# First loads of a two-layer decoder trunk issued at once; the squares of its first norm put behind the casts

## The chip, the cores and the metric

The kernel runs on one core of a Trainium2 chip. Its time is device time in microseconds (us) of one whole execution; lower is better. Three executions of the kernel before took 1265.56 us (median), 1262.03 us and 1266.27 us. A fourth, recorded by the hardware profiler, took 1263.57 us; from its first to its last recorded instruction, which is called the span, 1261.8 us pass.

## The reference, cut to what matters

The input x has 512 tokens of 1024 float32 values. Two layers work on it, each of them a token mixer with a residual and a squared-ReLU MLP (hidden size 4096) with a residual, and each of these starts with an RMSNorm:

```
def rmsnorm(x, g):
    y = x * rsqrt(mean(x * x, axis=-1) + EPS) * g
for layer in range(2):
    hn = rmsnorm(h, norm_mix[layer])
    h = h + mixer(hn, w_in[layer], ...)        # layer 0: even_mixer, layer 1: odd_mixer
    h = h + square(relu(rmsnorm(h, norm_mlp[layer]) @ w1)) @ w2
return rmsnorm(h, norm_final)
```

The change touches the very first rmsnorm and the first products of the even mixer: q, k and v of four heads of differential attention and eight heads of forgetting attention, all out of one projection `hn @ w_in`, with a rotary turn of q and k of the first group. The rest (attention, gates, output projections, the top-k attention of layer 1, the MLPs) is not changed.

## The kernel before

**Layout.** Everything is held transposed: 1024 features are 8 blocks of 128 partitions, each with 512 tokens (256 KB). A product in float32 is made of three TensorE passes over numbers that are split in two (a high part that the engine takes as it is, and the rest as a low part): high times high, high times low, low times high (L325, L326, L327). One output block of 128 columns is 8 such triples over the feature blocks, 24 matmuls of 128x128 by 128x512, into one bank of PSUM called `pg`; three such banks exist (`B_PG`).

**Weights.** All weights lie in one packed array in the order in which they are used. `stage` (L250) writes the plan. `emit_split` (L257; its load is L264) takes the next entry of the plan: at the first column block of an entry it loads the raw weights on SyncE's queue into one of two `raw` buffers (512 KB for an entry of 128 columns), then ScalarE makes the high part (L160, a cast) and VectorE the low part (L161, a subtraction) into one of three `whl` buffers. `wnext` calls it one block ahead of use.

**The first norm.** `first_norm` (L225 on) loads the blocks of x (tiles `hx`), splits the first weights in two halves, and calls `norm`. For each feature block j, `norm` makes the high part of x times the norm's gain on ScalarE (L202) and the low part on VectorE (L203), lets the first product go on by a step (`step`), and then squares an earlier block on ScalarE (L209, L212) and adds the square up on VectorE (L213). The factor of rmsnorm itself is not needed for the product: it is multiplied in later. From the sum of squares, eight small matmuls (L166), VectorE (L169), GpSimd's power (L171) and VectorE (L218, L176) make a diagonal matrix, two matmuls (L189, L190) spread it over the partitions, ScalarE copies it to `r_b` (L220), and VectorE multiplies the rotary tables `csr` by it (L223). Only then can the first product's bank `pg` be read out (L360, L361) and be used for the fourth output block.

**Before the first norm** TensorE runs `WARM` matmuls on a tile of ones (L130) whose result nothing reads.

**Order.** The program is written in the order above, but a planner of the framework fixes the order of each engine's instructions at build time: by its own costs it walks through time, and of the instructions whose inputs it takes to be ready on an engine, it puts the one that the program names first. The engines then run that fixed order, each one strictly in line. DMA issues of a queue stand in the same line as the engine's own work: the queue of ScalarE carries x blocks of odd number, `cols` and `ident`; that of SyncE the even ones, the weights and `csr`. The framework has a small number of completion counters for these DMAs, so that a late issue first waits until an earlier DMA has landed.

Of the kernel before, what the change touches and what calls it, by code (L numbers as in the profile page):

```python
# [13 lines left out]
AF = mybir.ActivationFunctionType  # L14
# [7 lines left out]
KB = D // P  # L22
# [27 lines left out]
V_FIRST = 2  # L50
DVE_ODD = 6
DVE_EVEN = 6
WARM = 8
PAD = 320
SHUF = list(range(8, 16)) + list(range(0, 8)) + list(range(16, 32))
OFF = [P * t * (t + 1) // 2 for t in range(NT + 1)]
# [22 lines left out]
def trunk(ctx, tc, packs, b_forget, lambda_q1, lambda_k1, lambda_q2, lambda_k2, rope, eye, xT, vecs, wpk, out):  # L79
    nc = tc.nc  # L80
# [7 lines left out]
    def blk(tag, bufs, shape=(P, S), dt=F32, pool=None):  # L88
        tile_n[0] += 1
        return (pool or big).tile(list(shape), dt, name=f"{tag}_{tile_n[0]}", tag=tag, bufs=bufs)  # L90
# [9 lines left out]
    scr = lambda: blk("scr", 5)  # L100
# [5 lines left out]
    h = [lpool.tile([P, S], F32, name=f"hx{j}") for j in range(KB)]  # L106

    def load_x(j, q=None):
        (q or nc.sync).dma_start(h[j], xT[j * P:(j + 1) * P])
# [18 lines left out]
    busy = pO()  # L128
    for i in range(WARM):
        nc.tensor.matmul(busy, onesf[:, :P], onesf, start=True, stop=True)  # L130
    nhalf = const.tile([P, NT], F32, name="nhalf")
    nc.gpsimd.memset(nhalf, -0.5)
    csr = const.tile([P, 2, S], F32, name="csr")
# [25 lines left out]
    def split(dst_hi, dst_lo, src, eng=None):  # L159
        nc.scalar.copy(dst_hi, src)  # L160
        (eng or nc.vector).tensor_sub(dst_lo, src, dst_hi.bitcast(F32))  # L161

    def rsqrt_cols(sq, inv_n, ts=range(NT)):
        p = pT()
        for t in ts:
            nc.tensor.matmul(p[:, t:t + 1], sq[:, t * P:(t + 1) * P], ones1, start=True, stop=True)  # L166
        c = slice(ts[0], ts[-1] + 1)
        v = small(4)
        nc.vector.tensor_scalar(v[:, c], p[:, c], inv_n, EPS, op0=OP.mult, op1=OP.add)  # L169
        r = small(4)  # L170
        nc.gpsimd.tensor_tensor(r[:, c], v[:, c], nhalf[:, c], op=OP.pow)  # L171
        return r
# [19 lines left out]

    rtm = const.tile([P, NT], F32, name="rtm")

    def norm(gcol, rope_tab, step=None, lag=0):
        gh = []
        acc = scr()
        for j in range(KB):
            hi = blk("gh", 16, dt=F32R)
            lo = blk("gh", 16, dt=F32R)  # L200
            g = cols[:, gcol + j:gcol + j + 1]
            nc.scalar.activation(hi, h[j], AF.Copy, scale=g)  # L202
            nc.vector.scalar_tensor_tensor(lo, h[j], g, hi.bitcast(F32), op0=OP.mult, op1=OP.subtract)  # L203
            gh.append((hi, lo))
            if step:
                step(gh)
            for i in range(max(j - lag, 0) if j >= lag else KB, j - lag + 1 if j < KB - 1 else KB):
                if i == 0:
                    nc.scalar.activation(acc, h[i], AF.Square)  # L209
                else:  # L210
                    sq = scr()
                    nc.scalar.activation(sq, h[i], AF.Square)  # L212
                    nc.vector.tensor_add(acc, acc, sq)  # L213
        r_tables(rsqrt_cols(acc, 1.0 / D), rope_tab)
        return gh

    def r_tables(r, rope_tab):
        nc.vector.tensor_copy(rtm, r)  # L218
        p = bcast_cols(r)
        nc.scalar.copy(r_b, p)  # L220
        if rope_tab:
            for i in range(2):
                nc.vector.tensor_mul(csr[:, i], csr[:, i], r_b)  # L223

    def first_norm(w, c0):  # L225

        load_x(1, nc.scalar)
        emit_split(2)
        for j in range(2, KB):
            load_x(j, nc.scalar if j % 2 else nc.sync)  # L230
        nc.sync.dma_start(csr, rope.rearrange("a p s -> p a s"))
        nc.scalar.dma_start(ident, eye)
        pout = pg()
        wt = ready.pop(0)[0]
        gen = []

        def step(gh):
            if not gen:
                gen.append(gemm_steps(pout, wt, gh))
                return  # L240
            next(gen[0])

        gh = norm(0, True, step, 2)
        for _ in gen[0]:
            pass
        return gh, pout

    plan, ready = [], []
# [5 lines left out]

    raws = {}

    def emit_split(parts=1):  # L257
        w, r0, c0, c, n, wd, lo, at = plan.pop(0)
        ks = [slice(i * KB // parts, (i + 1) * KB // parts) for i in range(parts)]
        if c == 0:  # L260
            raw = blk("raw", RAW_BUFS, (P, KB * WC), F32, wts)[:, :KB * wd]
            src = wpk[at:at + D * wd].rearrange("(p f) -> p f", p=P)
            for k in ks:
                nc.sync.dma_start(raw[:, k.start * wd:k.stop * wd], src[:, k.start * wd:k.stop * wd])  # L264
            raws[0] = raw.rearrange("p (k c) -> p k c", c=wd)
        t = blk("whl", WHL_BUFS, (P, 2, KB, P), F32R, wts)
        for k in ks:
            split(t[:, 0, k, :n], t[:, 0, k, n:2 * n] if n == 8 else t[:, 1, k, :n], raws[0][:, k, c:c + n], lo)
        ready.append((t, w, r0, c0 + c))

    def wnext(w, r0, c):
        while plan and len(ready) <= AHEAD:
            emit_split()
        t, w_, r_, c_ = ready.pop(0)
        assert (w_, r_, c_) == (w, r0, c)
        return t
# [44 lines left out]
    def gemm_steps(pout, wt, rhs, n=P, start=True, stop=True, ks=range(KB)):  # L321
        for k, (a, b) in enumerate(rhs):
            if k not in ks:
                continue
            nc.tensor.matmul(pout, wt[:, 0, k, :n], a, start=start and k == 0, stop=False)  # L325
            nc.tensor.matmul(pout, wt[:, 0, k, :n], b, start=False, stop=False)  # L326
            last_mm[0] = nc.tensor.matmul(pout, wt[:, 1, k, :n], a, start=False, stop=stop and k == KB - 1)  # L327
            yield
# [306 lines left out]
    def h_reload(ap):  # L635
        r = [blk("h", KB, pool=ap) for j in range(KB)]
        for j in range(KB):
            nc.sync.dma_start(r[j], hd[j])
        return r
# [11 lines left out]
    def mlp(ap, layer, done=None):  # L651
        gh = norm(16 + KB * layer, False)
        half = 2 * D
        w1, w2 = ("w_mlp_in", layer), ("w_mlp_out", layer)
        for f0 in range(0, D_FF, half):
            acts = []
            def fin(p, put):
                t = blk("t", 3, pool=ap)
                nc.vector.scalar_tensor_tensor(t, p, 0.0, r_b, op0=OP.max, op1=OP.mult)  # L659
                hi = blk("act", 32, dt=F32R, pool=ap)  # L660
                lo = blk("act", 32, dt=F32R, pool=ap)
                nc.scalar.activation(hi, t, AF.Square)
                sq = blk("t", 3, pool=ap)
                nc.scalar.activation(sq, t, AF.Square)
                nc.vector.tensor_sub(lo, sq, hi.bitcast(F32))
                put((hi, lo))

            for s in range(half // WC):
                acts += proj(w1, gh, f0 + s * WC, fin)
            out_gemm(w2, f0, acts, done if f0 + half == D_FF else None)  # L670
# [149 lines left out]
    def odd(ap, gh):  # L820
# [119 lines left out]
        return early.finish(obs)  # L940

    gh, p0 = first_norm(("w_in_even", 0), 0)
    load.__exit__(None, None, None)
    with tc.tile_pool(name="even", bufs=1, reuse_waits="tile") as ap:
        om, pe = even(ap, gh, p0)
    with tc.tile_pool(name="mlp0", bufs=1, reuse_waits="tile") as ap:
        blk("pad", 1, (P, PAD // 4), pool=ap)
        h = [blk("h", KB, pool=ap) for j in range(KB)]
        for j in range(KB):
            load_x(j)  # L950
        out_gemm(("w_out_even", 0), 0, om, early=pe)
        mlp(ap, 0)
        nc.scalar.dma_start(csr, rope.rearrange("a p s -> p a s"))
        gh = norm(KB, True)
        h_spill()
    with tc.tile_pool(name="odd", bufs=1, reuse_waits="tile") as ap:
        om, pe = odd(ap, gh)
    with tc.tile_pool(name="mlp1", bufs=1, reuse_waits="tile") as ap:
        blk("pad", 1, (P, PAD // 4), pool=ap)
        h = h_reload(ap)  # L960
# [48 lines left out]
```

## Time and profile before

| what | us |
|---|---|
| median of three runs | 1265.56 |
| the profiled execution | 1263.57 |
| its span | 1261.8 |
| TensorE matmuls busy | 1242.1 |
| VectorE busy | 719.8 |
| ScalarE busy | 558.9 |
| GpSimd busy | 97.6 |

Busy times add up the time in which an engine has an instruction in work. They are read as shares of the span: TensorE is at 98%. What an engine other than TensorE does counts only where TensorE waits for it, so that the stretches in which TensorE stands still, or runs at its lower clock, are what there is to read.

### The profile page before, as it was taken

The numbers are of one execution on the slowest core, as the hardware profiler recorded it, in microseconds if no ns is written. First come the engines' busy times: TensorE is split into PE (matmuls) and PEld (weight loads), VectorE is DVE, ScalarE is ACT, GpSimd is POOL, SyncE is SP. The second block draws the span as 40 slices with busy tenths as digits, with TensorE's granted clock in tenths as the row PEclk, the third lists the DMA queues.
The fourth block names the chain that finished last, engine by engine and source line by source line (L and its number), as shares of the span: only waits on it lengthen the run. The fifth ranks groups of instructions, "written<-read, shape, count | busy, mean of one in ns | idle before, by whom it ended". The sixth has DMA issues, their size and how long they took to land.

```text
span 1261.8 us, 15425 instructions
## 1 busy us (share of the span) xinstructions
PE 1242.1 (98%) x5856; PEld 1026.8 (81%) x5856; DVE 719.8 (57%) x1359; ACT 558.9 (44%) x1014; POOL 97.6 (8%) x68
## 2 busy tenths in 40 slices
PE   7999999999999999999999999999999999999997
PEld 5878888888888888888788888877888888888887
DVE  6887659664432244434499987787644322444232
ACT  5456667444421134323353578885533222333231
POOL 2000000000000000000114533230000000000000
PEclk9999999999999999999999999999999999999999
DMA  6546342322222222233334344523322222222211
GB/s 184 144 120 166 96 142 73 121 100 100 101 101 89 85 94 100 101 117 110 134 100 152 96 124 118 152 79 134 100 101 90 88 92 98 100 100 100 101 67 67
DMA packets 36298, 136.82 MB, mean 108 GB/s; under 512 B 5440, under 2 KB 5568, under 8 KB 26240
## 3 DMA queue, kind: packets, MB, share of 16 engines
q1 hardware_dynamic: 34784, 133.52, 32.5%
q10 hardware_dynamic: 1136, 1.66, 0.4%
q0 software_dynamic: 304, 0.66, 0.4%
q8 instruction: 46, 0.75, 0.2%
q14 instruction: 28, 0.23, 0.1%
HBM read 111.18 MB, written 4.19 MB: 91 GB/s over the span
## 4 chain that ended last, share of the span: by engine, by line
PE 88%; DVE 5%; ACT 3%; DMA 2%; issue 1%; POOL 0%; SPq 0%; POOLq 0%; DVEq 0%; ACTq 0%
PE pg L325 26%; PE pg L326 26%; PE pg L327 26%; PE pT L484 2%; PE pS L450 1%; PE pS L451 1%; DMA raw<-in_wpk_dram 1%; PE pO L503 1%; PE pO L502 1%; DMA hx<-in_xT_dram 1%; DVE whl L161 1%; ACT P L458 1%; PE pT L166 1%; DVE P L456 1%; PE pT L419 1%
## 5 line engine op out<-in xcount | busy, mean ns | idle before, releaser
L160 ACT CAST whl<-raw 128x1024 fp32r<-128x1024 f32 (+1 forms) x199 | 206.8, 1041 | 534.4 <-PE pg L327 484.9
L325 PE MATMUL pg<-gh,whl 128*128 128x512 f32 x1064 | 421.8, 397 | 5.1 <-ACT gh L202 3.7
L326 PE MATMUL pg<-gh,whl 128*128 128x512 f32 x1064 | 416.7, 392 | 1.0 <-DVE gh L203 0.9
L327 PE MATMUL pg<-gh,whl 128*128 128x512 f32 x1064 | 416.3, 392 | 0.6 <-DVE whl L161 0.6
L161 DVE TENSOR_TENSOR whl<-raw,whl 128x1024 fp32r<-128x1024 f32 (+2 forms) x175 | 211.5, 1209 | 181.1 <-ACT whl L160 180.9
L325 PEld LDWEIGHTS pg<-gh,whl 128*128 128x128 f32 x1064 | 200.0, 188 | 44.5 <-ACT gh L202 4.9
L327 PEld LDWEIGHTS pg<-gh,whl 128*128 128x128 f32 x1064 | 199.9, 188 | 42.3 <-DVE whl L161 1.0
L326 PEld LDWEIGHTS pg<-gh,whl 128*128 128x128 f32 x1064 | 200.1, 188 | 41.9 <-DVE gh L203 3.8
L325 PE MATMUL pg<-act,whl 128*128 128x512 f32 (+1 forms) x528 | 202.1, 383 | 0.0
L327 PE MATMUL pg<-act,whl 128*128 128x512 f32 (+1 forms) x528 | 202.0, 383 | 0.0
L326 PE MATMUL pg<-act,whl 128*128 128x512 f32 (+1 forms) x528 | 202.0, 383 | 0.0
L659 DVE SCALAR_TENSOR_TENSOR t<-pg,r_b 128x512 f32<-128x512 f32 x64 | 44.3, 691 | 156.1 <-PE pg L327 153.6
L325 PEld LDWEIGHTS pg<-act,whl 128*128 128x128 f32 x528 | 99.2, 188 | 19.5
L327 PEld LDWEIGHTS pg<-act,whl 128*128 128x128 f32 x528 | 99.2, 188 | 19.3
L326 PEld LDWEIGHTS pg<-act,whl 128*128 128x128 f32 x528 | 99.2, 188 | 19.2
L458 ACT ACTIVATE P<-P,sm 128x128 f32<-128x128 f32 (+3 forms) x128 | 71.7, 561 | 48.9 <-DVE sm L456 48.5
L612 DVE TENSOR_TENSOR h<-h,pg 128x512 f32<-128x512 f32 x46 | 31.3, 686 | 106.6 <-PE pg L327 106.6
L161 POOL TENSOR_TENSOR whl<-raw,whl 128x1024 fp32r<-128x1024 f32 x24 | 57.8, 2408 | 122.2 <-ACT whl L160 100.6
L171 POOL TENSOR_TENSOR sm<-sm,nhalf 128x4 f32<-128x4 f32 (+1 forms) x10 | 12.3, 1225 | 656.8 <-DVE sm L169 656.8
L161 DVE TENSOR_TENSOR PT<-pT,PT 128x384 fp32r<-128x384 f32 (+1 forms) x84 | 49.8, 597 | 19.9 <-ACT PT L160 19.3
L160 ACT CAST PT<-pT 128x384 fp32r<-128x384 f32 (+1 forms) x84 | 42.4, 510 | 14.3 <-PE pT L484 13.8
L484 PE MATMUL pT<-ident,P 128*128 128x128 f32 x280 | 46.5, 275 | 1.8 <-ACT P L471 0.9
(198 smaller groups left out, 1163.4 us busy)
## 6 DMA issues: line engine op xcount, KB each, us to landing
raw<-in_wpk_dram SPq DMA_DIRECT2D x78, 1024.0 KB, 4.8
raw<-in_wpk_dram SPq DMA_DIRECT2D x39, 512.0 KB, 3.9
qk<-qk SPq DMA_DIRECT2D x156, 128.0 KB, 2.3
h<-in_xT_dram SPq DMA_DIRECT2D x8, 256.0 KB, 4.7
hd<-h SPq DMA_DIRECT2D x8, 256.0 KB, 2.0
h<-hd SPq DMA_DIRECT2D x8, 256.0 KB, 4.8
out_dram<-y SPq DMA_DIRECT2D x4, 512.0 KB, 3.0
hx<-in_xT_dram SPq DMA_DIRECT2D x4, 256.0 KB, 9.0
```

The costliest lines, as they stand in the source:

```text
L160: nc.scalar.copy(dst_hi, src)
L161: (eng or nc.vector).tensor_sub(dst_lo, src, dst_hi.bitcast(F32))
L166: nc.tensor.matmul(p[:, t:t + 1], sq[:, t * P:(t + 1) * P], ones1, start=True, stop=True)
L325: nc.tensor.matmul(pout, wt[:, 0, k, :n], a, start=start and k == 0, stop=False)
L326: nc.tensor.matmul(pout, wt[:, 0, k, :n], b, start=False, stop=False)
L327: last_mm[0] = nc.tensor.matmul(pout, wt[:, 1, k, :n], a, start=False, stop=stop and k == KB - 1)
L419: nc.tensor.transpose(q[:, t * P:(t + 1) * P], y[:, t * P:(t + 1) * P], ident)
L450: nc.tensor.matmul(sp[m][:, c], qb[m][:, q], kb[0][m][:, :w], start=True, stop=False)
L458: nc.scalar.activation(o, o, AF.Exp, bias=st[m][:, t:t + 1], scale=-1.0, accum_out=st[m][:, 4 + t:5 + t])
L484: nc.tensor.transpose(p[:, o - o0 + (t - kt) * P:o - o0 + (t - kt + 1) * P], pt[:, OFF[t] + kt * P:OFF[t] + (kt + 1) * P], ident)
L612: nc.vector.tensor_add(h[j], h[j], p)
L659: nc.vector.scalar_tensor_tensor(t, p, 0.0, r_b, op0=OP.max, op1=OP.mult)
```

## The change

All loads of x and the first two halves of weights are issued ahead of the first split (`fetch` is the loading part of `emit_split`, and does nothing when it has been done). The first split's casts come behind the high part of x block 0. Within `step`, the second weights are split after the last block of x, and the load of the rotary tables is issued behind that. With `lag`, all squares come in a loop of their own behind these. Two of the eight warming matmuls go.

```diff
-WARM = 8
+WARM = 6
+    def squares(acc, j):
+        if j == 0:
+            nc.scalar.activation(acc, h[j], AF.Square)
+        else:
+            sq = scr()
+            nc.scalar.activation(sq, h[j], AF.Square)
+            nc.vector.tensor_add(acc, acc, sq)
+
-    def norm(gcol, rope_tab, step=None, lag=0):
+    def norm(gcol, rope_tab, step=None, lag=False):
...
             if step:
                 step(gh)
-            for i in range(max(j - lag, 0) if j >= lag else KB, j - lag + 1 if j < KB - 1 else KB):
-                if i == 0:
-                    nc.scalar.activation(acc, h[i], AF.Square)
-                else:
-                    sq = scr()
-                    nc.scalar.activation(sq, h[i], AF.Square)
-                    nc.vector.tensor_add(acc, acc, sq)
+            if not lag:
+                squares(acc, j)
+        for j in range(KB if lag else 0):
+            squares(acc, j)
         r_tables(rsqrt_cols(acc, 1.0 / D), rope_tab)
...
     def first_norm(w, c0):
-        load_x(1, nc.scalar)
-        emit_split(2)
-        for j in range(2, KB):
+        fetch(2)
+        for j in range(1, KB):
             load_x(j, nc.scalar if j % 2 else nc.sync)
-        nc.sync.dma_start(csr, rope.rearrange("a p s -> p a s"))
         nc.scalar.dma_start(ident, eye)
         pout = pg()
-        wt = ready.pop(0)[0]
         gen = []
         def step(gh):
-            if not gen:
+            j = len(gh)
+            if j == 1:
+                emit_split(2)
+                wt = ready.pop(0)[0]
                 gen.append(gemm_steps(pout, wt, gh))
                 return
             next(gen[0])
-        gh = norm(0, True, step, 2)
-        for _ in gen[0]:
-            pass
+            if j == KB:
+                next(gen[0])
+                emit_split()
+                nc.sync.dma_start(csr, rope.rearrange("a p s -> p a s"))
+        gh = norm(0, True, step, True)
...
+    def fetch(parts=1):
+        w, r0, c0, c, n, wd, lo, at = plan[0]
+        if c == 0 and fetched[0] != at:
+            fetched[0] = at
...
     def emit_split(parts=1):
+        fetch(parts)
         w, r0, c0, c, n, wd, lo, at = plan.pop(0)
```

## Rows read from the trace of the kernel before

**Rows 1.** The page's first part: busy time of each engine, share of the span, instructions.

```profile
PE 1242.1 (98%) x5856; PEld 1026.8 (81%) x5856; DVE 719.8 (57%) x1359; ACT 558.9 (44%) x1014; POOL 97.6 (8%) x68
```

**Rows 2.** Stretches: start to end and length; busy time per engine (instructions), clock, DMA, GB/s.

```profile
9.03:19.50 10.47, 9.43 (x24) 5.60 (x25) 9.88 (x16) 10.07 (x17) 1.65 (x3) 1.00 0.71 251
19.50:24.48 4.98, 3.63 (x19) 2.50 (x17) 3.93 (x6) 0.96 (x2) 1.90 (x1) 1.00 0.25 72
```

**Rows 3.** Waits, 0 to 60 us: who waited for whom, total us, times, longest.

```profile
PE pg L325 <- ACT gh L202: 3.7, 1, 3.7
...
PE pT L189 <- ACT scr L160: 0.8, 1, 0.8
...
PE pg L327 <- DVE whl L161: 0.6, 1, 0.6
```

**Rows 4.** Timeline of ScalarE: start, duration, line, out<-in, count, [idle before <- ended by].

```profile
7.16 0.62 ACT L160 CAST whl<-raw 128x512 fp32r<-128x512 f32 x1 [1.76 <-DMA raw<-in_wpk_dram]
...
8.25 0.72 ACT L202 ACTIVATE gh<-hx,cols 128x512 fp32r<-128x512 f32 x1 [0.48 <-issue]
8.88 0.61 ACT L209 ACTIVATE scr<-hx 128x512 f32<-128x512 f32 x1
...
17.86 1.98 ACT L160 CAST whl<-raw 128x1024 fp32r<-128x1024 f32 x2
```

**Rows 5.** DMAs issued at 0.74, 1.18, 1.65, 2.12, 7.16, 10.53: us to landing last.

```profile
hx<-in_xT_dram SPq DMA_DIRECT2D x1, 256.0 KB, 2.8
raw<-in_wpk_dram SPq DMA_DIRECT2D x1, 256.0 KB, 3.6
raw<-in_wpk_dram SPq DMA_DIRECT2D x1, 256.0 KB, 5.5
hx<-in_xT_dram SPq DMA_DIRECT2D x1, 256.0 KB, 8.4
hx<-in_xT_dram ACTq DMA_DIRECT2D x1, 256.0 KB, 8.6
raw<-in_wpk_dram SPq DMA_DIRECT2D x1, 512.0 KB, 6.9
```

**Rows 6.** Timeline of VectorE, columns as in rows 4.

```profile
11.51 0.74 DVE L203 SCALAR_TENSOR_TENSOR gh<-hx,cols,gh 128x512 fp32r<-128x512 f32 x1
...
18.12 0.75 DVE L203 SCALAR_TENSOR_TENSOR gh<-hx,cols,gh 128x512 fp32r<-128x512 f32 x1
18.79 0.68 DVE L213 TENSOR_TENSOR scr<-scr,scr 128x512 f32<-128x512 f32 x1
...
20.80 1.23 DVE L161 TENSOR_TENSOR whl<-raw,whl 128x1024 fp32r<-128x1024 f32 x1
...
29.75 0.68 DVE L361 TENSOR_TENSOR scr<-pg,csr 128x512 f32<-128x512 f32 x1
```

**Rows 7.** Timeline of TensorE's matmuls, columns as in rows 4.

```profile
1.52 3.78 PE L130 MATMUL pO<-onesf 128*128 128x512 f32 x8 [1.52 <-DVE onesf L125]
...
9.03 0.79 PE L325 MATMUL pg<-gh,whl 128*128 128x512 f32 x1 [3.73 <-ACT gh L202]
...
13.39 0.63 PE L325 MATMUL pg<-gh,whl 128*128 128x512 f32 x1
13.82 0.44 PE L326 MATMUL pg<-gh,whl 128*128 128x512 f32 x1
...
19.50 0.39 PE L325 MATMUL pg<-gh,whl 128*128 128x512 f32 x1
...
24.48 0.50 PE L189 MATMUL pT<-scr,onesr 128*128 128x512 f32 x1 [0.75 <-ACT scr L160]
...
33.47 0.39 PE L327 MATMUL pg<-gh,whl 128*128 128x512 f32 x1
33.70 0.39 PE L325 MATMUL pg<-gh,whl 128*128 128x512 f32 x1
```

**Rows 8.** Waits of SyncE's queue, 0 to 60 us, columns as in rows 3.

```profile
SPq L264 <- DMA hx<-in_xT_dram: 3.4, 1, 3.4
```

More of the change, by code (lines that the diff above doesn't have):

```diff
@@ L255, in trunk, with emit_split @@
     raws = {}
[L257 to L260, printed above, removed]
+    def fetch(parts=1):
+        w, r0, c0, c, n, wd, lo, at = plan[0]
+        if c == 0 and fetched[0] != at:
+            fetched[0] = at
             raw = blk("raw", RAW_BUFS, (P, KB * WC), F32, wts)[:, :KB * wd]
             src = wpk[at:at + D * wd].rearrange("(p f) -> p f", p=P)
-            for k in ks:
-                nc.sync.dma_start(raw[:, k.start * wd:k.stop * wd], src[:, k.start * wd:k.stop * wd])
+            for k in range(parts):
+                f = slice(k * KB * wd // parts, (k + 1) * KB * wd // parts)
+                nc.sync.dma_start(raw[:, f], src[:, f])
             raws[0] = raw.rearrange("p (k c) -> p k c", c=wd)
+    fetched = [-1]
+    def emit_split(parts=1):
+        fetch(parts)
+        w, r0, c0, c, n, wd, lo, at = plan.pop(0)
         t = blk("whl", WHL_BUFS, (P, 2, KB, P), F32R, wts)
-        for k in ks:
+        for i in range(parts):
+            k = slice(i * KB // parts, (i + 1) * KB // parts)
             split(t[:, 0, k, :n], t[:, 0, k, n:2 * n] if n == 8 else t[:, 1, k, :n], raws[0][:, k, c:c + n], lo)
```

## The prediction

> **What bounds the kernel now.** The page comes first: TensorE's matmuls fill 1242.1 us, 98% of the span, so some 20 us are to be had on it, and every other engine is below 60% [rows 1]. The change touches the first 20 us and nothing behind them, so the next view is the stretches and the waits of the start. Between the first real matmul (9.03) and the end of the first product (19.50), ScalarE is busy 10.07 and VectorE 9.88 of 10.47 us: they set the pace here, not TensorE. From 19.50 to 24.48 TensorE is busy 3.63 of 4.98 us [rows 2]. Its waits name three causes: 3.7 us for the first high part of x, 0.6 us for the low part of the second weights, 0.8 us for the cast in the chain of the norm [rows 3].
>
> Why the first high part is late is seen on ScalarE: it stands at 8.25 behind the cast of the second half of the weights, which waited for its load until 7.16 [rows 4]. The load of x block 0 had landed at 0.74 + 2.8 = 3.5, the two halves of the weights at 1.18 + 3.6 = 4.8 and 1.65 + 5.5 = 7.1, x block 2 only at 2.12 + 8.4 = 10.5, x block 7 at 7.16 + 8.6 = 15.8, the second weights at 10.53 + 6.9 = 17.4 [rows 5]. VectorE then alternates a low part and an addition: six low parts start between 11.51 and 18.12, one each (18.12 - 11.51) / 5 = 1.32 us, and the sum of squares ends at 18.79 + 0.68 = 19.47 [rows 6]. The second weights' subtraction comes last, 20.80 to 22.03, and TensorE waits for it. The point by which I judge the whole start is the first matmul of the fourth output block: 33.70 [rows 7]. It needs the first bank back, which VectorE releases at 29.75 + 0.68 = 30.43 [rows 6]. So there are 33.70 - 30.43 = 3.27 us between the chain of the norm and TensorE's path: what TensorE gains up to that block is capped near 3.3 us unless the chain comes earlier too. From 33.47 to 33.70 one matmul takes 0.23 us, the pace of the rest [rows 7].
>
> **The change part by part.**
>
> *First high part in front of the casts.* ScalarE can start on x block 0 at about 3.8 (block 0 has landed, `cols` is awaited as well) in place of 8.25. The first cast can follow its load at 4.8, with 0.62 for the cast [rows 4] and about 0.7 for a subtraction of 512 columns (the addition of that size takes 0.68, [rows 6]): first matmul near 6.2, 2.8 us earlier. This is hardly worth anything by itself. TensorE does blocks 0 and 1 (six matmuls of 0.43 at the pace from 13.39 to 13.82, [rows 7]), is done near 8.8, and then waits for block 2. That load does not move: it was issued at 2.12 and is behind the same bytes. High part 0.72 [rows 4]: the low part of block 2 starts at 10.5 + 0.7 = 11.2, where it was 11.51. Gain so far 0.3 us. ScalarE's queue may put a load that waits for a counter ahead of the first high part; the last candidate frees at 7.1 (the second half's landing), and TensorE would do blocks 0 and 1 until about 10.8, still ahead of block 2's low part: 0.
>
> *x loads earlier.* The four odd blocks no longer wait behind casts. If blocks 4 to 7 (1.05 MB) move behind 10.5 at the mean 251 GB/s of this stretch [rows 2], the last lands at 14.7, between 10.5 and the old 15.8. At VectorE's pace its low part is not wanted before 11.2 + 5 x 1.32 = 17.8, or 17.6 without the small waits: 0 to 0.3 us more. I take 0.1.
>
> *Squares behind all.* The source puts them last, but the planner fills an engine when it takes the next block not to have landed. Before, a square stands right behind the first high part (8.88, [rows 4]) although the source had two more high parts ahead of it. So I expect high part and square, low part and addition to alternate again, and the first product to end near 19.1 (19.50 - 0.4).
>
> *Second weights' split ahead of the squares, their load ahead of the rotary tables.* The load was issued at 10.53 and waited 3.4 us for a counter [rows 8]; put right behind x block 6 it lands no later than 17.4, and one 512 KB load at 251 GB/s (2.1 us) earlier at best. The cast comes to ScalarE between 15.5 and 17.9, and the subtraction to VectorE right behind the last low part (18.4) or one addition later (19.1). It takes 1.23 [rows 6]: end 19.6 to 20.3 in place of 22.03, saving 1.7 to 2.4 us of TensorE's second product. That is the main term; I take 2.0.
>
> *What the norm's chain gives back.* The same subtraction now stands in front of the last additions: sum of squares at 19.47 - 0.4 + 1.15 = 20.2. The spread (L189) started at 24.48 [rows 7], 5.0 us behind the sum, and TensorE had waited for it [rows 3]; it would now start near 25.2, while TensorE comes by 2 us earlier. Its place in TensorE's line is fixed by the planner. If the planner puts enough matmuls of the second product ahead of it, this costs 0; if its place stays, the whole gain and 0.7 us are lost. The planner also sees the weights earlier, so I take the end near 0: 0.4 us.
>
> *Parts at nothing.* The rotary tables (512 KB) are issued later; they are first multiplied within the 5.95 us between 24.48 and 30.43, and landing by 17.4 + 2.1 = 19.5 leaves 5 us of cover. Without that cover each us late would be a us on the bank's release. Two warming matmuls less: eight took 3.78 us [rows 7], and TensorE stands idle behind them in any case.
>
> Sum: 0.4 + 2.0 - 0.4 - 0.4, the last for waits that the planner's new order makes further back, is 1.6 us. The profiled execution took 1263.57, so 1262.0. It lies 2.0 below the median; the four executions shown have a mean of 1264.4, and it is this that I carry the sum to: 1262.7.
>
> **The rivals.**
>
> *The planner really puts the squares behind (B).* Then a low part needs only its own 0.75. The last one ends at 16.2 (landing 14.7, high part 0.72, low part 0.75), and TensorE sets the pace: from 11.2 at 0.43 per matmul, 4.8 us long as before (9.03 to 13.82, where the pace goes up, [rows 7]), then 0.23: first product done at 17.6, second and third 48 x 0.227 = 10.9 and about 1.4 for the small ones: 29.9, a gain of 3.8. The additions end near 20.5, and 10.96 behind that (30.43 - 19.47) the bank is free: 31.5, a gain of 2.2, or more if some squares go early. I put it at 1260.5 on the same base. For it: the source's order. Against it: the square at 8.88.
>
> *Hidden anyway or taken back (C).* L189 keeps its place, or TensorE's clock rises late. The row first: eight matmuls of 0.43 from 1.52 to 5.30 did not bring the higher pace, and after 3.7 us without work TensorE began at 0.43 again, which is the level of 1.2 GHz, though the column of the clock shows 1.00 throughout [rows 2, 7]. Now it idles from about 8.8 to 11.2; if the rise comes another 4.8 us later than the 16.0 above, at 20.8, some four or five matmuls of the second product cost 0.2 us more each: 0.9 us. Then the gain is between 0 and 1.6 - 0.9 = 0.7; I take 0.5, a time of 1263.9.
>
> By the Trainium skill, "TensorE: Matmul & The Clock Gate", section "Part 1: The HAM clock gate", the half rate is what an idle engine returns to and sustained activity releases it. By that rule a start broken by a wait for block 2 keeps the lower clock longer, which is the loss of rival C; rows of before show only the unbroken start.
>
> *Slower (D): the chain of the norm becomes the path.* If ScalarE's line holds the second weights' cast (and the third's) in front of most squares, it stands for the load until 15 to 17.4, then casts 1.0, or 2.0 for two (17.86, 1.98, [rows 4]), then eight squares of 0.61 [rows 4] = 4.9: 20.9 to 24.3, and the last addition ends 0.8 later, at 21.7 to 25.1. The bank is free 10.96 later. It decides from a sum later than 33.70 - 10.96 = 22.7 on; at 25.1 the fourth block starts at 36.1, 2.4 us late. Rotated q and k, and with them the first scores, come as late. 1264.4 + 2.4 = 1266.8. For it: the order of the source; against it: squares of landed blocks fill ScalarE's line while it waits, as before.
>
> **How the numbers follow.** Forecast 0.42, B 0.26, C 0.18, D 0.14. About 0.3% (3.8 us) is what a measurement of this kernel can tell from no change. Faster by more: half or more of B, and the upper tails of the forecast, which a new order throughout the attention stage may widen: 0.30. Slower by more: most of D: 0.12. Within: 0.58. The forecast's own range is 0 to 3 us of gain, 1261.4 to 1264.4; with B, part of D and the 4.2 us by which executions of before differ, 1258.5 to 1266.5.
>
> **What would show it.** The first matmul near 6 us; a gap in TensorE before 11; high parts and squares alternating (forecast) or not (B); the subtraction of the second weights ending near 20; the fourth block starting near 32. The prediction is wrong if block 2 of x lands well before 10.5, if L189's wait grows by 2 us, or if the sum of squares ends after 22.7.

## The result, and the profile after

The changed kernel takes 1270.82 us (median of five, 1269.39 to 1270.99) against 1264.27 us of the kernel before (five, 1262.03 to 1266.27): a ratio of 1.0051, 95% interval 1.0034 to 1.0067. It is slower by 6.5 us. The forecast was 1262.7 us and the range ended at 1266.5: the time lies above both. The profiled executions, 1269.39 us and 1263.57 us, are 5.8 us apart, and so are their spans.

The page after, its first part:

```profile
span 1267.6 us, 15426 instructions
PE 1243.9 (98%) x5854; PEld 1029.2 (81%) x5854; DVE 720.1 (57%) x1359; ACT 559.2 (44%) x1014; POOL 96.3 (8%) x68
```

TensorE has nearly the same number of matmuls as in [rows 1], and its busy time grew by 1.8 us. Two stretches show where; columns as in [rows 2], the clock being the number behind the five engines. First after, then before:

```profile
34.00:43.00 9.00, 5.36 (x14) 4.20 (x14) 8.82 (x17) 2.29 (x3) 0.00 (x0) 0.65 0.49 146
...
60.00:100.00 40.00, 39.59 (x201) 31.18 (x199) 35.27 (x100) 21.56 (x49) 0.00 (x0) 1.00 0.36 101
```

```profile
34.00:43.00 9.00, 9.00 (x42) 7.44 (x41) 9.00 (x22) 2.23 (x4) 0.00 (x0) 1.00 0.66 152
...
60.00:100.00 40.00, 38.69 (x198) 30.21 (x197) 35.82 (x99) 22.53 (x51) 0.00 (x0) 1.00 0.50 134
```

From 34 to 43 us TensorE was fully busy before; now it does 14 matmuls in place of 42, stands still for 3.6 us, and its granted clock is 0.65. From 60 to 100 it gets 0.9 us back: 0.4 us of waits are left of 1.3. TensorE's timeline after shows the wait and the slow matmuls behind it (columns as in [rows 4]):

```profile
8.73 0.79 PE L341 MATMUL pg<-gh,whl 128*128 128x512 f32 x1 [4.29 <-ACT whl L160]
...
15.73 1.42 PE L341 MATMUL pg<-gh,whl 128*128 128x512 f32 x2 [2.50 <-ACT whl L160]
...
33.61 0.40 PE L343 MATMUL pg<-gh,whl 128*128 128x512 f32 x1
37.64 0.79 PE L341 MATMUL pg<-gh,whl 128*128 128x512 f32 x1 [3.64 <-DVE scr L377]
38.23 0.63 PE L342 MATMUL pg<-gh,whl 128*128 128x512 f32 x1
...
43.35 0.46 PE L342 MATMUL pg<-gh,whl 128*128 128x512 f32 x1
43.65 0.39 PE L343 MATMUL pg<-gh,whl 128*128 128x512 f32 x1
```

The last matmul of the third product starts at 33.61, only 0.14 later than in [rows 7]. Then TensorE waits 3.64 us for VectorE to read out the first bank, and the fourth block starts at 37.64 in place of 33.70: 3.94 us. Behind the wait its first 14 matmuls take 43.65 - 37.64 = 6.01 us, 0.43 each, the pace of the 1.2 GHz level; fourteen at 0.23 take 3.2. Together: 3.94 + 2.8, less the 0.9 from 60 to 100 us, and 0.2 more for waits between 43 and 60 us, is 6.0 us; the spans differ by 5.8.

Why is the bank late? VectorE after:

```profile
15.71 1.23 DVE L161 TENSOR_TENSOR whl<-raw,whl 128x1024 fp32r<-128x1024 f32 x1 [3.97 <-ACT whl L160]
16.85 0.75 DVE L211 SCALAR_TENSOR_TENSOR gh<-hx,cols,gh 128x512 fp32r<-128x512 f32 x1
...
21.91 0.75 DVE L211 SCALAR_TENSOR_TENSOR gh<-hx,cols,gh 128x512 fp32r<-128x512 f32 x1
22.57 0.68 DVE L201 TENSOR_TENSOR scr<-scr,scr 128x512 f32<-128x512 f32 x1
23.17 1.22 DVE L738 TENSOR_TENSOR pick<-ident 128x1024 fp32r<-128x1024 f32 x1
24.31 0.68 DVE L201 TENSOR_TENSOR scr<-scr,scr 128x512 f32<-128x512 f32 x1
24.91 1.22 DVE L161 TENSOR_TENSOR whl<-raw,whl 128x1024 fp32r<-128x1024 f32 x1
26.05 0.68 DVE L201 TENSOR_TENSOR scr<-scr,scr 128x512 f32<-128x512 f32 x1
...
36.91 0.68 DVE L377 TENSOR_TENSOR scr<-pg,csr 128x512 f32<-128x512 f32 x1
```

The sum of squares ends at 26.05 + 0.68 = 26.73, where it was 19.47 [rows 6], and the bank is free 10.86 later, at 37.59 (before 10.96 later). So the whole delay, 7.26 us, arises in front of the sum. It has two parts. The last low part of x ends at 22.66 in place of 18.87: 3.79 us. And three additions are left behind the last low part, where it was one, with `pick` (a mask that the top-k layer needs much later) and the third weights' subtraction between them, so that 4.07 us pass between the last low part and the sum, where it was 0.60: 3.47 us.

The first part comes from ScalarE:

```profile
7.45 0.72 ACT L210 ACTIVATE gh<-hx,cols 128x512 fp32r<-128x512 f32 x1 [4.77 <-issue]
...
10.25 0.71 ACT L210 ACTIVATE gh<-hx,cols 128x512 fp32r<-128x512 f32 x1
14.63 1.04 ACT L160 CAST whl<-raw 128x1024 fp32r<-128x1024 f32 x1 [3.67 <-DMA raw<-in_wpk_dram]
15.58 0.72 ACT L210 ACTIVATE gh<-hx,cols 128x512 fp32r<-128x512 f32 x1
```

The cast of the second weights stands between the third and the fourth high part of x. ScalarE waits 3.67 us for that load with x block 3 behind it. Two answers of the DMA view tell when the loads landed, of issues near 1.7 us (ScalarE's queue, x block 3) and at 5.87 us (SyncE's queue, the second weights); the last column is us from issue to landing:

```profile
hx<-in_xT_dram ACTq DMA_DIRECT2D x1, 256.0 KB, 6.1
...
raw<-in_wpk_dram SPq DMA_DIRECT2D x1, 512.0 KB, 8.7
```

Block 3 was there at 7.8, the weights at 14.6. About half a us of the 3.79 arises on VectorE: the fourth high part ends at 16.30, but the subtraction of the second weights stands in front of its low part, which starts at 16.85.

### The profile page after: what moved, and what is told of

It reads as the page before. It is cut to its first block, busy times and chain, and to the rows that moved or that the text cites. A ratio compares the mean times of both kernels' runs of the same rounds, so it can differ in the third digit from the quotient of the medians.

```text
span 1267.6 us, 15426 instructions
## 1 busy us (share of the span) xinstructions
PE 1243.9 (98%) x5854; PEld 1029.2 (81%) x5854; DVE 720.1 (57%) x1359; ACT 559.2 (44%) x1014; POOL 96.3 (8%) x68
## 4 chain that ended last, share of the span: by engine, by line
PE 91%; DVE 3%; ACT 2%; DMA 1%; issue 1%; SPq 0%; POOL 0%; POOLq 0%; DVEq 0%; ACTq 0%
PE pg L341 27%; PE pg L343 27%; PE pg L342 27%; PE pT L500 2%; PE pS L466 1%; PE pS L467 1%; DMA raw<-in_wpk_dram 1%; PE pO L519 1%; PE pO L518 1%; PE pT L166 1%; ACT P L474 1%; PE pT L435 1%; ACT whl L160 0%; DVE whl L161 0%; DVE P L472 0%
```

## The experiments

Theory T: the place of the cast in ScalarE's line costs the time (it delays the high parts, these the sum, the sum the bank, and TensorE's wait for the bank brings the lower clock). Rival R: what costs is the squares' new place, or the loads' collisions, and the cast's place is a side effect. Times are medians; the ratio is to the kernel before on the same chip, with its 95% interval.

**The cast held back (e2_held).** The changed kernel, with the second split ordered behind the last high and low part:

```diff
-                emit_split()
+                with tc.issue_after(last_x[0].ins), tc.issue_after(last_x[1].ins):
+                    emit_split()
```

> The changed kernel, with one thing different: the cast and the subtraction of the second weights are held behind the last high and low part of x. Theory (the cast of the second weights stands in ScalarE's line ahead of five high parts and waits for its load until 14.6 us): the high parts follow their loads again, the last low part ends near 18.5, the sum of squares near 20.3 in place of 26.7, the first bank is free near 31, TensorE waits less than 1 us for it and keeps its higher clock: 1261 to 1264 us. Rival (it is the loop of squares behind everything that makes the sum late): the squares still stand last in the source, so the sum stays near 26 and the time near 1270.8.

1261.72 us, ratio 0.9978 (0.9969 to 0.9986). ScalarE, VectorE, then TensorE:

```profile
17.82 1.04 ACT L160 CAST whl<-raw 128x1024 fp32r<-128x1024 f32 x1
```

```profile
20.49 0.68 DVE L202 TENSOR_TENSOR scr<-scr,scr 128x512 f32<-128x512 f32 x1
```

```profile
32.37 0.40 PE L343 MATMUL pg<-gh,whl 128*128 128x512 f32 x1
```

None has a wait in front of it. The squares and loads stand as the change put them, the last low part ends at 18.83, the sum at 21.17, and the fourth block starts 1.3 us earlier than before. Moving this one split turned the loss into a gain of 2.8 us: T holds, and R falls as the main cause.

**The squares back in their old order (e3_old_squares).** The changed kernel, with square j-2 behind block j:

```diff
-        for j in range(KB if lag else 0):
-            squares(acc, j)
+            elif j >= 2:
+                for i in range(j - 2, j - 1 if j < KB - 1 else KB):
+                    squares(acc, i)
```

> The changed kernel, with the squares back in their old places (two blocks behind, the last three behind the last block). The second weights' cast now stands between the last two high parts in ScalarE's line, and the last three additions stand behind other work of VectorE (the selector, the third weights' subtraction). Theory: the cast no longer waits, the last low part ends near 19.5, the sum near 24 for the additions that are held up, the bank is free near 34, a wait of 1 to 3 us: 1264 to 1267.5. Rival (squares alone are to blame): with them back, as before or better, 1262 to 1264.

1261.61 us, 0.9977 (0.9969 to 0.9986): below what T expected. The number alone would speak for R, but the planner had moved the cast as well, to between the seventh and the eighth high part, where it waits for nothing:

```profile
16.11 1.05 ACT L160 CAST whl<-raw 128x1024 fp32r<-128x1024 f32 x1
17.07 0.72 ACT L210 ACTIVATE gh<-hx,cols 128x512 fp32r<-128x512 f32 x1
```

```profile
32.03 0.50 PE L342 MATMUL pg<-gh,whl 128*128 128x512 f32 x1 [0.57 <-DVE scr L378]
```

So this run doesn't separate the two. It shows two other things. In the changed kernel it takes both edits, the split named early and the squares named behind it, to bring the cast in front of the fourth high part (e1_load_only, below, takes back the other one). And additions behind `pick` and a subtraction (4.1 us from the last low part to the sum, as after) cost only 0.57 us of waiting here, where the low parts were on time.

**The cast early in the kernel before (e7_cast_early).** The kernel before, whose squares and loads stay, with the second split named after the third block of x:

```diff
             next(gen[0])
+            if len(gh) == 3:
+                emit_split()
```

> The kernel before, with one thing added: the second weights are split right after the third block of x, so that their cast stands in ScalarE's line ahead of the fourth high part, as in the changed kernel; loads, squares and warming stay. Their load lands near 17.4 here. Theory: ScalarE stands until 17.4, the fourth high part moves from 11.7 to about 18.4, the last low part ends near 25, the fourth output block starts near 38: 1268 to 1271. Rival (squares, loads or the clock at the start make the loss): no change, 1264.3.

1266.57 us, 1.0019 (1.0010 to 1.0028), less than expected. ScalarE, VectorE, then TensorE:

```profile
17.09 1.04 ACT L160 CAST whl<-raw 128x1024 fp32r<-128x1024 f32 x1 [4.75 <-DMA raw<-in_wpk_dram]
```

```profile
36.74 0.68 DVE L363 TENSOR_TENSOR scr<-pg,csr 128x512 f32<-128x512 f32 x1
```

```profile
37.47 0.50 PE L327 MATMUL pg<-gh,whl 128*128 128x512 f32 x1 [1.61 <-DVE scr L363]
37.81 0.40 PE L328 MATMUL pg<-gh,whl 128*128 128x512 f32 x1
```

The cast's place alone, with the squares in their old order, makes the bank as late (37.42) and the fourth block nearly as late (3.77 us) as in the changed kernel; the load lands later here, so that no additions need be held up for it. It costs 2.1 us and not 6.5 mainly because the clock stays up: TensorE came to the wait later, waited 1.61 us, and the next matmuls run at 0.23. The rest adds up as after, 60 to 100 us giving back the same (busy 39.55 of 40): 3.77 - 0.9 - 0.2 (no waits from 43 to 60) = 2.7 against 2.5 between the spans.

**The wait filled with work (e4_filler).** The changed kernel with 15 matmuls, whose result nothing reads, behind the third product:

```diff
+        fill = pO()
+        for i in range(15):
+            with tc.issue_after(last_mm[0].ins):
+                nc.tensor.matmul(fill, onesr, gh[0][0], start=True, stop=True)
```

> The changed kernel, with 15 matmuls that nothing reads between the third and the fourth output block, in TensorE's line, where it waits 3.6 us for the first bank. They fill the wait (15 x 0.23 = 3.4 us) and move nothing else. Theory (the wait also drops TensorE to its lower clock, and 14 matmuls behind it take 0.43 in place of 0.23): the fourth block starts at the same 37.6 and runs at 0.23 from its start, 2.5 to 2.8 us less: 1268.1. Rival (only the wait counts, the slower matmuls are made up for by later waits): 1270.8, or more if the filler delays the fourth block.

1267.81 us, 1.0026 (1.0017 to 1.0035):

```profile
34.70 3.66 PE L810 MATMUL pO<-gh,onesr 128*128 128x512 f32 x15
38.51 0.50 PE L341 MATMUL pg<-gh,whl 128*128 128x512 f32 x1
38.84 0.40 PE L342 MATMUL pg<-gh,whl 128*128 128x512 f32 x1
...
41.83 0.39 PE L343 MATMUL pg<-gh,whl 128*128 128x512 f32 x1
```

The fourth block starts 0.9 us later than after, and the kernel is still 2 to 3 us faster (spans 2.2, medians 3.0): its first 14 matmuls take 41.83 - 38.51 = 3.32 us in place of 6.01. So 2.7 us of the loss is the clock. The 0.9 us are not the filler's: in this execution the third product ends as much later, and the bank is free at 38.45, 0.86 later than after. With 0.4 us less of waits from 43 to 60 us (busy 17.00 of 17), 2.7 + 0.4 - 0.9 is the 2.2 between the spans.

**The loads alone.** e1_load_only is the changed kernel whose second weights are loaded early and split where they were before; e13_loads_first is the kernel before with only the loads of the first weights and x put first.

```diff
-                emit_split()
+                fetch()
```

```diff
-        load_x(1, nc.scalar)
-        emit_split(2)
-        for j in range(2, KB):
+        emit_fetch(2)
+        for j in range(1, KB):
             load_x(j, nc.scalar if j % 2 else nc.sync)
...
+        emit_split(2)
```

> The changed kernel, with the second weights' load still issued early, and their cast and subtraction left to the place where the kernel before has them, behind the norm. All x parts, squares and additions now precede that cast. Theory (only the cast's place ahead of the high parts cost time): high parts follow their loads, the sum of squares ends near 19.5, the second product waits for the subtraction until about 21 to 22: 1261.5 to 1264. Rival (the loop of squares behind, or the early loads, also cost): above 1265.

> The kernel before, with only the loads moved: x and the first weights are all issued ahead of the first split; casts, squares, the second weights and warming stay. Theory: x block 2, which sets the pace, lands as before, so the loads alone give 0 to 1 us: 1263.5 to 1264.8. Rival (the loads are where e2_held's 2.8 us come from): 1262.

1264.22 us, 0.9989 (0.9979 to 0.9999), and 1264.28 us, 1.0002 (0.9993 to 1.0012). The loads in themselves are worth next to nothing, and harm nothing. In e1_load_only the second weights' subtraction starts at 20.78 (before 20.80 [rows 6]), and the fourth block is where it was:

```profile
33.65 0.39 PE L341 MATMUL pg<-gh,whl 128*128 128x512 f32 x1
```

This run also keeps the squares' new place, the loop behind all blocks, so that it answers the other half of R: squares and loads together cost nothing while the cast stays behind the high parts. The squares' loop alone in the kernel before was not run.

**The small rows out of the way.** The five loads of small rows on GpSimd's queue (`bf`, four `lq`, 132 KB in all) run between the first blocks of x. They are issued behind GpSimd's power of the first norm here, in the kernel before (e8_rows_late), in the changed one (e9b_after_rows_late) and in e2_held (e9_held_rows_late):

```diff
-    nc.gpsimd.dma_start(bf, ...)
-    for i, a in enumerate((lambda_q1, lambda_k1, lambda_q2, lambda_k2)):
-        nc.gpsimd.dma_start(lq[:, i], ...)
+    def row_loads():
+        with tc.issue_after(last_pow[0].ins):
+            nc.gpsimd.dma_start(bf, ...)
+            for i, a in enumerate((lambda_q1, lambda_k1, lambda_q2, lambda_k2)):
+                nc.gpsimd.dma_start(lq[:, i], ...)
...
     gh, p0 = first_norm(("w_in_even", 0), 0)
+    row_loads()
```

> The kernel before, with one thing different: the five loads of small rows on GpSimd's queue (b_forget and four lambda rows, 128 times the same 32 or 256 bytes each) are issued behind the norm's power in place of at 1.4 us; nothing needs them before 37 us. Theory (their packets hold the DMA engines between 5 and 10 us, where 34 to 300 GB/s move at a full share of the engines): x block 2 lands near 8 in place of 10.5, the second half of the first weights near 5.5, first matmul near 7.5, the first product 1 to 1.5 us earlier: 1262.8 to 1263.8. Rival (the rate there is set by something else): loads land as before, 1264.4.

> The changed kernel with only the small rows loaded late; the lines of ScalarE, VectorE, TensorE and SyncE keep the changed kernel's order, with the second weights' cast ahead of the fourth high part. Theory (what that cast costs is the lateness of its load, and the wait of TensorE with the lower clock behind it): the load lands near 11.5 to 12 in place of 14.6, the sum of squares 2.6 us earlier, the fourth block near 35 in place of 37.6, and with a wait under 2.5 us TensorE may keep its higher clock: 1264 to 1267. Rival (the place in the line costs by itself, and late rows give the 2 us that they gave elsewhere): 1268.8.

> The changed kernel with the second weights' split held behind the last x part (e2_held) and the small rows loaded late. Theory: the first product in e2_held is paced from x block 2's landing at 10.5 on; with that near 8, the whole chain (low parts, sum, release of the first bank) comes 1.5 to 2.5 us earlier: 1259 to 1260.5. Rival: VectorE or the bank's release sets the end all the same: 1261.7.

e8_rows_late: 1262.52 us, 0.9981 (0.9972 to 0.9989). Stretches of the start, the last two columns being the DMA engines' busy share and GB/s; first the kernel before, then e8_rows_late:

```profile
5.00:7.50 2.50, 0.30 (x1) 0.00 (x0) 0.69 (x1) 0.74 (x2) 0.00 (x0) 1.00 1.04 151
7.50:10.00 2.50, 0.97 (x2) 0.47 (x3) 1.58 (x3) 2.02 (x4) 0.12 (x1) 1.00 0.99 198
```

```profile
5.00:7.50 2.50, 0.30 (x1) 0.00 (x0) 1.30 (x3) 1.58 (x3) 0.00 (x0) 1.00 1.06 379
7.50:10.00 2.50, 2.12 (x4) 1.32 (x5) 1.97 (x5) 2.50 (x5) 1.27 (x3) 1.00 0.96 346
```

At about the same busy share the DMA engines move 1.7 to 2.5 times as much; x block 2 lands 5.0 us after its issue, not 8.4 [rows 5].

e9b_after_rows_late, whose engines have the order of the changed kernel: 1266.20 us, 1.0016 (1.0007 to 1.0024), against 1268.89 us of the changed kernel run beside it (after_again, 1.0041, 1.0029 to 1.0053, with the trace of the first run again).

> The changed kernel once more, beside the others on this chip: 1270.8, and the same waits.

```profile
11.52 1.04 ACT L165 CAST whl<-raw 128x1024 fp32r<-128x1024 f32 x1 [2.01 <-DMA raw<-in_wpk_dram]
```

```profile
34.84 0.79 PE L346 MATMUL pg<-gh,whl 128*128 128x512 f32 x1 [3.64 <-DVE scr L382]
35.43 0.63 PE L347 MATMUL pg<-gh,whl 128*128 128x512 f32 x1
```

With the same order and an earlier landing, the fourth block comes 2.71 us earlier than in after_again (37.55), and the time is 2.69 us shorter. The expected range was met only because the changed kernel took 1268.89 us here and not 1270.8; the gain is nearer to the rival's 2 us than to the 4 to 7 that the theory gave. That the clock stays up did not come: TensorE is earlier too, waits as long, and falls to 0.43.

e9_held_rows_late: 1260.01 us, 0.9960 (0.9947 to 0.9972), as expected; the two gains add up (fourth block at 30.72). It differs from e9b_after_rows_late in the place of the split alone, and the ratios, each to the kernel before on its own chip, are 0.0056 apart, some 7 us: with the small rows out of the way the cast's place costs as much as before.

**Additions on GpSimd (e10_pool_adds).** e9_held_rows_late with three of the additions of squares on GpSimd:

```diff
+            if j <= 4:
+                nc.gpsimd.tensor_add(other, other, sq)
+            else:
+                nc.vector.tensor_add(acc, acc, sq)
+        nc.vector.tensor_add(acc, acc, other)
```

> As e9_held_rows_late, and three of the seven additions of squares go to GpSimd with a sum of its own. Theory (VectorE alternates low part and addition at 1.27 us a block and so paces the first product): low parts follow each other at 0.67 as soon as x is there, TensorE paces the first product, 1 to 2 us less than e9_held_rows_late. Rival (x's landing or the chain behind the sum is what counts, or GpSimd slows VectorE): equal to e9_held_rows_late or slower.

1262.27 us, 0.9977 (0.9968 to 0.9987): slower than without. VectorE, then GpSimd:

```profile
12.08 4.70 DVE L231 SCALAR_TENSOR_TENSOR gh<-hx,cols,gh 128x512 fp32r<-128x512 f32 x3 [0.38 <-ACT gh L230]
```

```profile
11.52 4.71 POOL L218 TENSOR_TENSOR scr<-scr,scr 128x512 f32<-128x512 f32 x3 [10.39 <-ACT scr L216]
```

Three low parts took 1.57 us each beside it, not 0.74. The sum came 3.85 us later than in e9_held_rows_late (23.35 against 19.50), but only 0.97 of that lies in front of the last low part (it ends at 18.13, there at 17.16). The rest is again VectorE's order: two subtractions and `pick` stand between the last low part and the sum, where e9_held_rows_late has one subtraction. The last low part and the last addition:

```profile
17.39 0.74 DVE L231 SCALAR_TENSOR_TENSOR gh<-hx,cols,gh 128x512 fp32r<-128x512 f32 x1
...
22.67 0.68 DVE L221 TENSOR_TENSOR scr<-scr,scr 128x512 f32<-128x512 f32 x1
```

So this run does not tell what the slower low parts cost by themselves.

**The best version (e11_best).** e9_held_rows_late, with `ident` loaded on SyncE's queue behind the second weights, and the second half of the first weights cast behind the second high part:

```diff
-        nc.scalar.dma_start(ident, eye)
...
+            if j == 3:
+                split_half(1)
             if j == 1:
-                emit_split(2)
+                split_half(0)
...
                     emit_split()
+                nc.sync.dma_start(ident, eye)
```

> As e9_held_rows_late, and: the identity is loaded behind the second weights on SyncE's queue, so that ScalarE's line reaches the first high part without waiting for a counter, and the second half of the first weights is cast behind the second high part. Theory: first high part near 4, block 2's high part near 8.4 in place of 9.35, everything behind it 0.5 to 1 us earlier: 1259 to 1259.6. Rival (the last additions of the squares now stand behind the selector and a subtraction, the sum comes later and the bank with it): 1260 to 1262.

1258.84 us, 0.9960 (0.9947 to 0.9973): 5 us faster than the kernel before, 10 faster than the changed one beside it. ScalarE, then TensorE:

```profile
5.04 0.72 ACT L216 ACTIVATE gh<-hx,cols 128x512 fp32r<-128x512 f32 x1 [2.36 <-DMA raw<-in_wpk_dram]
...
7.31 0.72 ACT L216 ACTIVATE gh<-hx,cols 128x512 fp32r<-128x512 f32 x1
```

```profile
29.87 0.50 PE L363 MATMUL pg<-gh,whl 128*128 128x512 f32 x1 [0.54 <-DVE scr L399]
```

Its fourth block is 0.85 us earlier than in e9_held_rows_late, but the two ratios are the same: the runs don't tell these two apart. Two things were changed at once here, so the gain of neither is known.

## Why the prediction was wrong

*The step that failed:* "The cast comes to ScalarE between 15.5 and 17.9, and the subtraction to VectorE right behind the last low part". The time was nearly right, 14.63, and the place was wrong: the cast stood in ScalarE's line in front of the fourth high part, and the subtraction in front of the fourth low part. I had put both behind the last block because the source does, though the same text said that the planner fills an engine with whatever it takes to be ready. That rule had to be applied to the new load: issued at 5.87 in place of 10.53, it looks ready early, and the squares, which used to fill ScalarE while it waited for x, are now named behind the cast. That the planner took the load to be there before block 3 is argued from the order; that either edit taken back moves the cast away is shown (e1_load_only, e3_old_squares), and so is what the place costs (e2_held, e7_cast_early).

*What the norm's chain gives back, 0.4 us.* It gave back 3.94. The rows by which this can be followed were read rightly: the cover of 3.27 us in front of the fourth block (7.16 us of delay at the bank, less 3.27, is 3.89), and about 11 us from the sum to the bank. The sum of squares was wrong, 26.73 against a forecast 20.2, and beyond the 22.7 that the prediction itself named as a sign of being wrong. The other sign at the norm's chain, a longer wait in front of L189, did not come: TensorE had other matmuls to do there and waited at the bank.

*Rival D* was what happened, with a chance of 0.14. "If ScalarE's line holds the second weights' cast (and the third's) in front of most squares, it stands for the load until 15 to 17.4": it stood until 14.63. Its argument against itself, that squares of landed blocks fill the line, fell with the naming. It was also too small, 1266.8 us, in three terms. Five high parts stood behind the cast, not only squares. The last additions came behind `pick` and a subtraction; these two together put the fourth block at 37.64, not 36.1 at most. And what the clock costs behind the wait, 2.7 us, was not in it at all. I had weighed the clock only at its first rise. The Trainium skill, "TensorE: Matmul & The Clock Gate", section "HAM oscillation — how this bites in real kernels", says that a wait between two bursts of matmuls lets the array fall back, so that the next burst starts slow. The traces of after and of e9b_after_rows_late agree (0.43 behind 3.64 us); that of e7_cast_early, behind 1.61 us, shows no fall.

*Rivals B and C.* The squares did not go behind all high parts (B). TensorE's pace did rise late, as C had it, for another reason: it had risen at 12.5, fell to 0.43 again behind the wait of 2.50 us for the same cast, and rose at 19.5 (13.8 before). That cost nothing, since the third product ended only 0.14 us later and the bank came later still.

*First high part at 3.8, first matmul near 6:* 7.45 and 8.73. Three issues, of two x loads and `ident`, held ScalarE's line from 3.78 to 7.4; that they waited for counters is argued from their length. The text had named this and priced it at 0. It can't be what made the loss, since e2_held has the same loads, starts at 7.63 and gains. e11_best, which takes `ident` off that queue among other things, starts at 5.04.

*x block 2 at 10.5, unmoved:* 9.5 (2.12 + 7.4); ScalarE came to its high part only at 10.25. *Squares and high parts alternate:* right from the fourth high part on. *Rotary tables, warming matmuls at nothing:* nothing showed against it; the tables landed at 16.2 and were first used at 33.69.

*The main term, 2.0 us from the second weights' subtraction,* is to be had where the order is the one I assumed, in e2_held: it starts at 19.36 in place of 20.80, the fourth block 1.3 us earlier, the time 2.8 us lower (1.8 between the profiled spans), where I had put 1.6. Even there the sum of squares ends at 21.17, not 20.2. In the changed kernel the gain was had as well: from 20 to 34 us TensorE was busy 13.94 us in place of 12.65, but this only made good for the late first product.

*Waits further back, 0.4 us against:* they came with the other sign, 0.9 us less between 60 and 100 us. The sum itself has a slip without weight: 1264.4 less 1.6 is 1262.8, not 1262.7.

What stays open: why 0.9 us come back between 60 and 100 us. It is one wait of TensorE for VectorE in the attention, 1.3 us before and 0.4 after. The late fourth block is not the reason: e2_held, where that block is early, is busy for 39.60 of the 40 us too, and e1_load_only, where it is in its old place, for 39.93.

## What to carry to other kernels

Before an instruction that waits for a load is named earlier in an order that a planner fixes, ask what the planner will take as ready at that point and what then stands behind it on its engine: a cast in a strict line turns one late transfer into a late everything. Price a wait of TensorE with the low pace behind it, not only with its own length. And before loads are moved, look at GB/s beside the DMA engines' busy share: here moving the large loads alone gave nothing (e13_loads_first), and moving five small ones out of their way gave 0.2% (e8_rows_late).

## What the runs showed of the hardware

- Behind a wait of 3.64 us TensorE did 14 matmuls at 0.43 us, granted clock 0.65 from 34 to 43 us; with fifteen matmuls of no use in that wait the next ones took 0.23. Behind 2.50 us (after, at 15.73) the pace fell to 0.43 too, behind 1.61 us (e7_cast_early) it did not.
- Five loads of small rows, 132 KB, hold down the rate of all loads beside them: 151 and 198 GB/s with them, 379 and 346 without, at a busy share near 1 in both.
- Low parts on VectorE and additions on GpSimd at the same time take 1.57 us each, on both engines; alone a low part takes 0.74. The Trainium skill, "SBUF — State Buffer", section "SBUF: two separate sides", says that the two engines take a shared pair of ports for a whole instruction and the other one blocks; the run agrees in that they hold each other up. That they work strictly in turns is not shown: no run has an addition on GpSimd alone, and the nearest row, GpSimd's subtraction of the same size in the kernel before (`vs`, 1.30 us), would make 0.74 + 1.30 = 2.04 us, not 1.57.
